# A decoder trunk in split float32 matmuls: five raw weight buffers for four, gate biases loaded into short-lived tiles, residual rows loaded in four portions

## The chip, the core and the metric

One core of a Trainium2 chip runs the whole kernel in one launch. The metric is the device time of one execution in microseconds (us); lower is better. TensorE (PE) multiplies matrices, VectorE (DVE), ScalarE (ACT) and GpSimd (POOL) do elementwise work, and SyncE (SP), ACT and POOL issue DMAs. Each engine runs its own instructions in the order in which they stand; semaphores hold an instruction until what it needs is there, and all that stands behind it on that engine waits too.

## The reference

The input `x` has 256 rows of 2048 channels (one batch, one layer), all in float32. What is computed:

```python
x = layer_norm(x, ln_in_g, ln_in_b)
z = x @ w_in                       # 2048 x 13312: a_b a_c a_h | b_u b_v | c_a c_g | g
gates = sigmoid(g + gate_bias).reshape(1, 256, 3, 2048)
y_a = a_b * causal_depthwise_conv(a_c * a_h, conv_a_w)              # 3 taps
y_b = b_u * (tril(sg_w) @ layer_norm(b_v) + sg_b)                   # chunks of 128 rows
y_c = silu(layer_norm(causal_depthwise_conv(c_a * sigmoid(c_g), cc_conv_w) + cc_conv_b))   # 31 taps
proj = stack([y_a, y_b, y_c]) @ w_branch                            # three of 1024 x 2048
mix = sum(gates * proj, over branches) @ w_out                      # 2048 x 2048
x = layer_norm(alpha * x + mix, ln_mix_g, ln_mix_b)
h_gate, h_up = split(x @ w_ffn_in)                                  # 2048 x 11264
ffn = (silu(h_gate) * h_up) @ w_ffn_out                             # 5632 x 2048
out = layer_norm(alpha * x + ffn, ln_ffn_g, ln_ffn_b)
```

The weights are read once, some 300 MB in all.

## The kernel before

**Tiles.** Every product has 256 rows of activations (two tiles `t` of 128) against weights that come in tiles of 128 x 1024 float32 (512 KB). A weight tile lands raw in `wraw` (L183, `RAW_BUFS` = 4 buffers). ScalarE copies it, rounded, to `whi` (L128), and VectorE takes the rest, `wlo` = `wraw` - `whi` (L130). Activations are split the same way into a high and a low part (`th`, `tl`; `yh`, `yl` for a branch's output). A product is three matmuls of 128 x 512: high by high, low by high, high by low (L251 to L253 in `gemm_block`, L205 to L207 in `gemm`). A raw buffer is free once its `wlo` is made; a split buffer (seven pairs, `SPLIT_BUFS`) once PE has used it. A plain step of one tile is 12 matmuls.

**Pairs.** In `gemm_block` some weight tiles are taken two at a time, with seven products in place of eight. For those, VectorE makes four sums of the two raw tiles first (`split_pair`, L142 to L153; in the trace L140, written to `tsum` and once back to `wraw`), and these are split too. The sums of the products (`tmp`) are put together on VectorE after the last pair (L296 to L299) and added to the other banks at the end of the block (`total`, L656).

**The order.** `plan` lists all 552 weight tiles in the order in which they are used. `pump(i)` (L192), called ahead of step `i`, records loads up to tile `i + DMA_AHEAD` and splits up to tile `i + SPLIT_AHEAD`. SP issues the loads, so the load of a tile waits on SP for the `wlo` of the tile four places earlier. Work that follows a block (transposes on PE into `th`, the gates, the residual) is put off by some steps with `defer`, whose clock counts steps, and runs between the steps of the next block; the causal convolution of branch C runs as background taps, two a step (L563). A scheduler then sets the final order on each engine.

**The places that matter here.** `branch` (L675) computes for each of three branches, in two halves, the gates (`gemm_block(("g", n, b))`) and the branch's projection (`("p", n, b)`). It loads two gate biases of 128 x 512 ahead of each gate block with DMAs on ACT's queue into `gb` (L681, two buffers of their own), adds them at the block's end (L685), and merges (`merged`, L702 to L705). `merged` is transposed (L310) for the output projection `("o", ...)`. Small row vectors are broadcast by POOL's DMAs into `tmp` tiles (`bcast`, L802 to L804); `tmp` is a pool of eight tiles of 128 x 512 that nearly all of the elementwise work shares. The rows of `x` for the residual are loaded again into `R` by eight POOL DMAs (`residual_rows`, L809 to L812), all recorded three steps into the `o` block, and `residual` (L820, L822) normalizes them there. `mix_residual` (L857, L858) does the like in the feed-forward part.

Of the kernel before, what the change touches and what calls it, by code (L numbers as in the profile page):

```python
# [8 lines left out]
F32 = mybir.dt.float32  # L9
# [3 lines left out]
ALU = mybir.AluOpType  # L13

P = 128
D = 2048
S = 256
NT = S // P
# [5 lines left out]
ALPHA = 2.0 ** 0.25  # L24
NW = 512
KT = 2
RAW_BUFS = 4
SPLIT_BUFS = 7
DMA_AHEAD = 5
SPLIT_AHEAD = 3  # L30
DEFER = 2
BACKGROUND = 2
# [9 lines left out]
SUMS_AT = 5  # L42
X_PAIRS = 2
LEAD = 6
ADDER = False

OFF_AB, OFF_AC, OFF_AH = 0, DA, 2 * DA
OFF_BU, OFF_BV = 3 * DA, 4 * DA
# [5 lines left out]
def trunk_kernel(ctx: ExitStack, tc: tile.TileContext, x, ln_in_g, ln_in_b, w_in, gate_bias,  # L54
                 conv_a_w, sg_ln_g, sg_ln_b, sg_w, sg_b, cc_conv_w, cc_conv_b, cc_ln_g, cc_ln_b,
                 w_branch, w_out, ln_mix_g, ln_mix_b, w_ffn_in, w_ffn_out, ln_ffn_g, ln_ffn_b, out):
    nc = tc.nc
# [6 lines left out]
    small = ctx.enter_context(tc.tile_pool(name="small", bufs=4))  # L64
# [10 lines left out]
    x2d = x.rearrange("b s d -> (b s) d")  # L75
    out2d = out.rearrange("b s d -> (b s) d")

    def cols(j, w=NW):
        return slice(j * w, (j + 1) * w)

    def new_tmp():
        return tmp.tile([P, NW], F32, name="tmp")
# [50 lines left out]
    def split_pair(t0, t1):  # L133


        b12, b11, b22, b21 = t0[:, 0, :], t0[:, 1, :], t1[:, 0, :], t1[:, 1, :]
        ts = wp.tile([P, 3, NW], F32, name="tsum", bufs=1)

        def add(out, a, b):
            nc.vector.tensor_tensor(out=out, in0=a, in1=b, op=ALU.add)  # L140

        add(ts[:, 0, :], b11, b12)  # L142
        if ADDER:
            nc.gpsimd.dma_start(out=b12, in_=b22, accum_op=ALU.add)
        else:
            add(b12, b12, b22)
        add(ts[:, 1, :], ts[:, 0, :], b22)
        second = split_tile(t1)
        if ADDER:
            nc.scalar.copy(out=ts[:, 2, :], in_=ts[:, 1, :])  # L150
            nc.gpsimd.dma_start(out=ts[:, 2, :], in_=b21, accum_op=ALU.add)
        else:
            add(ts[:, 2, :], ts[:, 1, :], b21)  # L153
        low = split_tile(ts[:, 0:2, :])
        first = split_tile(t0)
        last = split_tile(ts[:, 2:3, :], 1)

        def part(pair, i):
            return pair[0][:, i, :], pair[1][:, i, :]

        return {"b11": part(first, 1), "t3": part(first, 0), "b22": part(second, 0), "b21": part(second, 1),
                "t1": part(low, 0), "t2": part(low, 1), "t4": part(last, 0)}
# [18 lines left out]
    def load_one():  # L181
        j = state["dma"]
        t = wp.tile([P, KT, NW], F32, name="wraw", bufs=RAW_BUFS)  # L183
        nc.sync.dma_start(out=t, in_=plan[j])
# [7 lines left out]
    def pump(i):  # L192

        while state["dma"] < min(len(plan), i + 1 + DMA_AHEAD):
            while state["dma"] - state["split"] >= RAW_BUFS:
# [16 lines left out]
    def defer(fn, after=DEFER, banks=True):  # L212


        deferred.append((clock[0] + after, fn, banks))
# [36 lines left out]
        nc.tensor.matmul(ps, lhsT=ah, rhs=bl, start=False, stop=False)  # L252
        nc.tensor.matmul(ps, lhsT=al, rhs=bh, start=False, stop=last)  # L253

    def gemm_block(key, xs, evac, combos=None):

        steps = block[key]
        xh, xl = xs  # L260
        pairs = sum(kind == "pair" for kind, _, _ in steps)
        outs = {at: acc_bank() for at in ((0, 1), (1, 1), (0, 0), (1, 0))}
        adds, shared, free_at = {}, None, 0

        def a_of(k, t):
            return xh[:, k, cols(t, P)], xl[:, k, cols(t, P)]

        def c_of(i, c):
            return combos[0][:, c, i, :], combos[1][:, c, i, :]

        for s_, (kind, q, tile_) in enumerate(steps):
            pump(tile_)
            b = split_t.pop(tile_)
            first, last = s_ == 0, s_ == len(steps) - 1
            if kind == "one":
                hi, lo = b
                for i, ((t, n), ps) in enumerate(outs.items()):
                    product(ps, a_of(q, t), (hi[:, n, :], lo[:, n, :]), first, last)
                    if last:
                        evac(i, t, n, ps, adds.get((t, n)))  # L280
            else:
                if q == 0:
                    shared = [halves[1].tile([P, NW], F32, name="acc") for _ in range(4)]
                p1, p5, p6, p7 = shared
                st, sp = q == 0, q == pairs - 1
                product(outs[0, 1], a_of(2 * q + 1, 0), b["b21"], first, last)
                product(outs[0, 0], c_of(q, 3), b["b22"], first, last)
                product(p5, c_of(q, 0), b["t1"], st, sp)
                product(p6, c_of(q, 1), b["t2"], st, sp)
                product(p1, a_of(2 * q, 0), b["b11"], st, sp)  # L290
                product(p7, c_of(q, 2), b["t3"], st, sp)
                product(outs[1, 1], a_of(2 * q + 1, 1), b["t4"], first, last)
                if sp:
                    c1, u, r, v, w = (new_tmp() for _ in range(5))
                    nc.scalar.copy(out=c1, in_=p1)
                    nc.vector.tensor_tensor(out=u, in0=p6, in1=c1, op=ALU.add)  # L296
                    nc.vector.tensor_tensor(out=r, in0=p5, in1=u, op=ALU.subtract)
                    nc.vector.tensor_tensor(out=v, in0=u, in1=p7, op=ALU.subtract)
                    nc.vector.tensor_tensor(out=w, in0=p7, in1=r, op=ALU.add)  # L299
                    adds = {(0, 1): c1, (1, 1): v, (0, 0): r, (1, 0): w}  # L300
                    free_at = s_ + 3
            clock[0] += 1 if kind == "one" else 2
            run_deferred(shared is not None and not 0 < free_at <= s_ and not last)
        halves.reverse()
# [23 lines left out]
        nc.gpsimd.tensor_tensor(out=rs, in0=r, in1=mhalf, op=ALU.pow)  # L328
        return mv[:, 0:1], rs

    def stats_tile(name, n):
        return [small.tile([P, n, 6], F32, name=f"{name}{t}", bufs=1) for t in range(NT)]


    wi = w_in[0]
# [49 lines left out]
    xpool = xin.enter_context(tc.tile_pool(name="xpool", bufs=1))  # L385
# [76 lines left out]
    xT = new_xt(act)  # L462
# [5 lines left out]
    xTS = new_sums()  # L468
    x_kept = [blocks(xpool.tile([P, NW], F32, name=f"xk{t}")) for t in range(NT)]
    def x_stats(t):  # L470
        st = small.tile([P, 4, 6], F32, name="st", bufs=2)
        for q in range(4):
            nc.vector.bn_stats(out=st[:, q, :], in_=xt[t][:, cols(q)])
        return mean_rstd(st, mv_in[t], rs_in[t])
# [24 lines left out]
    brp = None  # L499
# [108 lines left out]


    vt = {(t, j): brp.tile([P, NW], F32, name="gate", bufs=4) for t in range(NT) for j in range(2)}  # L610
    bst = stats_tile("bst", 2)
    for j in range(2):
        def evac_bv(t, ps, j=j):
            nc.scalar.copy(out=vt[t, j], in_=ps)
# [60 lines left out]
    def branch(n, y, first, mT=None):  # L675
        for b in range(2):
            gates = {}
            gb = [brp.tile([P, NW], F32, name="gb", bufs=2) for _ in range(2)]
            for i in range(2):
                o = n * D + (2 * b + i) * NW  # L680
                nc.scalar.dma_start(out=gb[i], in_=gate_bias[0:1, o:o + NW].broadcast_to([P, NW]))  # L681

            def evac_g(i, t, h, ps, add):
                g = gates[t, h] = brp.tile([P, NW], F32, name="gate", bufs=4)
                nc.vector.tensor_tensor(out=g, in0=total(ps, add), in1=gb[h], op=ALU.add)  # L685
                nc.scalar.activation(out=g, in_=g, func=AF.Sigmoid)

            gemm_block(("g", n, b), xT, evac_g, xTS)
            if b == 1 and mT is not None:
                mT.extend(new_xt(act))  # L690
                mTS.extend(new_sums())
                later = late[:]
                late.clear()
                for i, f in enumerate(later):
                    f(DEFER + i)

            def evac_p(i, t, h, ps, add):
                j = 2 * b + h
                m = merged[t][:, cols(j)]
                z = gates[t, h]  # L700
                if first:
                    nc.vector.tensor_tensor(out=m, in0=ps, in1=z, op=ALU.mult)  # L702
                else:
                    nc.vector.tensor_tensor(out=z, in0=ps, in1=z, op=ALU.mult)
                    nc.vector.tensor_tensor(out=m, in0=m, in1=z, op=ALU.add)  # L705
                if mT is not None:
                    def move(after):
                        to_left(mT, mTS, j, t, m, after)
                    if b == 0:
                        late.append(move)  # L710
                    else:
                        move(DEFER + i)

            gemm_block(("p", n, b), y(), evac_p)
# [74 lines left out]
    R, x2T, xS = [], [], []  # L789
# [16 lines left out]

    stm = stats_tile("stm", 4)
    lg2, lb2 = (a.rearrange("(o d) -> o d", o=1) for a in (ln_in_g, ln_in_b))
    def residual_rows():  # L809
        for j in range(4):  # L810
            for t in range(NT):
                nc.gpsimd.dma_start(out=R[t][:, cols(j)], in_=x2d[cols(t, P), cols(j)])  # L812

    def residual(j, wait):
        gj, bj = bcast(lg2, j), bcast(lb2, j)
# [25 lines left out]
            for q in range((S_PAIRS + 1) // 2):  # L841
                defer(lambda q=q: token_sums(xS, 2 * q, kept[0, q], kept[1, q], min(2, S_PAIRS - 2 * q)), 6 + q, False)

    defer(residual_rows, 3, False)
    for j, at in enumerate((5, 7, 15, 17)):
        defer(lambda j=j: residual(j, 4), at, False)
    gemm_block(("o", 0), mT, lambda i, t, h, ps, add: evac_o(t, h, ps, add), mTS)
# [11 lines left out]
        defer(go, 3, False)  # L859


    stf = stats_tile("stf", 4)
    f_ln = {}

    def silu(ps, add=None):
# [96 lines left out]
```

## Time and profile before

| what | value |
|---|---|
| median of 3 runs | 1554.5 us (1552.83 to 1554.87) |
| the profiled execution's own time | 1554.82 us |
| its span, first to last instruction | 1553.1 us |
| PE busy | 1522.3 us, 98% |
| DVE, ACT, POOL busy | 1340.4 (86%), 771.2 (50%), 33.9 us (2%) |
| DMA | 308 MB, mean 198 GB/s |
| granted TensorE clock, mean | 0.995 |

A row of the timeline has the start, how long the instructions took, the engine, line, operation, what it writes and reads, a count and, in brackets, how long the engine stood idle before it and what ended that. `<-DMA wraw` means that a weight tile had not landed; `<-ACT whi` and `<-DVE wlo` that its high or low part was not made. The trace calls a buffer by its name in the kernel. An engine that is idle costs nothing unless PE, or the end, waits for it.

### The profile page before, as it was taken

Reading aid. Unit: us, or ns where it says so; the run is one execution under the profiler, and the core shown is the slowest. Engines: PE = TensorE matmul, PEld = TensorE weight load, DVE = VectorE, ACT = ScalarE, POOL = GpSimd, SP = SyncE. Lnnn points to the kernel's source line nnn. Section 1 sums busy time; section 2 is a strip of 40 time slices with the busy share of each in tenths; the row PEclk is TensorE's granted clock in tenths of the full one; section 3 lists DMA queues with packets and bytes.
Section 4 is the critical chain, followed back from the end, with each engine's and each line's share of the span. In section 5 each row is a group of like instructions: output and inputs, shape, how many; then the busy total and the mean of one; then the engine's idle time right before and its main releaser. Section 6 shows DMA issues by size and latency. Waiting matters only on the chain. (4 is left out here: it accounts for less than half of the span.)

```text
span 1553.1 us, 18820 instructions
## 1 busy us (share of the span) xinstructions
PE 1522.3 (98%) x6799; PEld 1246.5 (80%) x6799; DVE 1340.4 (86%) x1792; ACT 771.2 (50%) x885; POOL 33.9 (2%) x60
## 2 busy tenths in 40 slices
PE   7999999999999999999999999999999999999997
PEld 5888888888888888887877888788888878888885
DVE  7699999978789878787789799988899988888677
ACT  5544445444455454545436455555555554455451
POOL 1000000000000000000101000000000000000001
PEclk9999999999999999999999999999999999999998
DMA  6866556566664665756765666566665666666654
GB/s 221 271 190 189 183 153 227 169 216 205 197 204 156 213 204 185 243 170 201 235 208 182 203 190 216 177 227 207 190 189 176 203 193 198 206 190 202 217 180 145
DMA packets 103315, 308.13 MB, mean 198 GB/s; under 512 B 9908, under 2 KB 11028, under 8 KB 103222
## 3 DMA queue, kind: packets, MB, share of 16 engines
q1 hardware_dynamic: 98006, 293.29, 60.0%
q0 software_dynamic: 2560, 8.39, 1.9%
q10 hardware_dynamic: 2656, 5.26, 1.1%
q8 instruction: 53, 0.87, 0.2%
q14 instruction: 40, 0.33, 0.1%
HBM read 304.80 MB, written 2.10 MB: 198 GB/s over the span
## 5 line engine op out<-in xcount | busy, mean ns | idle before, releaser
L128 ACT CAST whi<-wraw 128x1024 fp32r<-128x1024 f32 x551 | 577.1, 1052 | 537.2 <-PE acc L253 165.7
L130 DVE TENSOR_TENSOR wlo<-wraw,whi 128x1024 fp32r<-128x1024 f32 x551 | 667.3, 1222 | 125.1 <-ACT whi L128 121.0
L251 PE MATMUL acc<-whi,th 128*128 128x512 f32 x1235 | 485.9, 393 | 1.9 <-ACT th L316 1.0
L252 PE MATMUL acc<-wlo,th 128*128 128x512 f32 x1235 | 481.7, 390 | 0.0
L253 PE MATMUL acc<-whi,tl 128*128 128x512 f32 x1235 | 481.1, 390 | 0.4 <-DVE tl L317 0.4
L251 PEld LDWEIGHTS acc<-whi,th 128*128 128x128 f32 x1235 | 231.9, 188 | 51.1 <-ACT th L316 1.4
L253 PEld LDWEIGHTS acc<-whi,tl 128*128 128x128 f32 x1235 | 231.7, 188 | 51.3 <-DVE tl L317 1.4
L252 PEld LDWEIGHTS acc<-wlo,th 128*128 128x128 f32 x1235 | 232.1, 188 | 47.8 <-DVE wlo L130 0.2
L205 PE MATMUL acc<-whi,th 128*128 128x512 f32 x496 | 195.4, 395 | 0.5 <-ACT whi L128 0.4
L206 PE MATMUL acc<-wlo,th 128*128 128x512 f32 x496 | 194.4, 393 | 1.6 <-DVE wlo L130 1.6
L207 PE MATMUL acc<-whi,tl 128*128 128x512 f32 x496 | 194.0, 392 | 0.0
L128 ACT CAST whi<-tsum 128x1024 fp32r<-128x1024 f32 x114 | 95.3, 836 | 145.4 <-DVE tsum L140 116.1
L130 DVE TENSOR_TENSOR wlo<-tsum,whi 128x1024 fp32r<-128x1024 f32 x114 | 108.7, 953 | 13.4 <-ACT whi L128 13.4
L206 PEld LDWEIGHTS acc<-wlo,th 128*128 128x128 f32 x496 | 93.5, 189 | 22.0 <-DVE wlo L130 3.0
L205 PEld LDWEIGHTS acc<-whi,th 128*128 128x128 f32 x496 | 93.6, 189 | 20.8 <-ACT whi L128 1.2
L207 PEld LDWEIGHTS acc<-whi,tl 128*128 128x128 f32 x496 | 93.6, 189 | 20.1 <-DVE tl L317 0.4
L563 DVE SCALAR_TENSOR_TENSOR cv<-pad,cw,cv 128x256 f32<-128x256 f32 x240 | 101.9, 489 | 0.0
L140 DVE TENSOR_TENSOR tsum<-tsum,wraw 128x512 f32<-128x512 f32 x114 | 78.2, 686 | 0.6
L251 PE MATMUL acc<-whi,yh 128*128 128x512 f32 x192 | 75.7, 394 | 0.0
L252 PE MATMUL acc<-wlo,yh 128*128 128x512 f32 x192 | 75.5, 393 | 0.0
L253 PE MATMUL acc<-whi,yl 128*128 128x512 f32 x192 | 74.7, 389 | 0.0
L140 DVE TENSOR_TENSOR tsum<-wraw 128x512 f32<-128x512 f32 x57 | 39.2, 688 | 32.6 <-DMA wraw<-in_w_in_dram 20.8
(164 smaller groups left out, 1191.1 us busy)
## 6 DMA issues: line engine op xcount, KB each, us to landing
wraw<-in_w_in_dram SPq DMA_DIRECT2D x208, 512.0 KB, 4.1
wraw<-in_w_ffn_in_dram SPq DMA_DIRECT2D x176, 512.0 KB, 4.3
wraw<-in_w_ffn_out_dram SPq DMA_DIRECT2D x88, 512.0 KB, 4.7
wraw<-in_w_branch_dram SPq DMA_DIRECT2D x48, 512.0 KB, 5.0
wraw<-in_w_out_dram SPq DMA_DIRECT2D x32, 512.0 KB, 6.4
gb<-in_gate_bias_dram ACTq DMA_DIRECT2D x12, 256.0 KB, 3.8
R<-in_x_dram POOLq DMA_DIRECT2D x8, 256.0 KB, 8.2
x<-in_x_dram SPq DMA_DIRECT2D x2, 512.0 KB
```

What stands on the lines that cost most here:

```text
L128: nc.scalar.copy(out=hi, in_=t)
L130: nc.vector.tensor_tensor(out=lo, in0=t, in1=hi.bitcast(F32), op=ALU.subtract)
L140: nc.vector.tensor_tensor(out=out, in0=a, in1=b, op=ALU.add)
L205: nc.tensor.matmul(ps, lhsT=xh[:, k, ts], rhs=hi[:, kk, :], start=first, stop=False)
L206: nc.tensor.matmul(ps, lhsT=xh[:, k, ts], rhs=lo[:, kk, :], start=False, stop=False)
L207: nc.tensor.matmul(ps, lhsT=xl[:, k, ts], rhs=hi[:, kk, :], start=False, stop=last)
L251: nc.tensor.matmul(ps, lhsT=ah, rhs=bh, start=first, stop=False)
L252: nc.tensor.matmul(ps, lhsT=ah, rhs=bl, start=False, stop=False)
L253: nc.tensor.matmul(ps, lhsT=al, rhs=bh, start=False, stop=last)
L563: nc.vector.scalar_tensor_tensor(out=cv[:, b, :], in0=pad[:, b, q:q + S], scalar=w_, in1=cv[:, b, :], op0=ALU.mult, op1=ALU.add)
```

## The change

`RAW_BUFS` goes from 4 to 5 and `DMA_AHEAD` from 5 to 6. The gate biases lose their own tiles `gb`: they are loaded into two `tmp` tiles by POOL's DMAs, recorded after the last pair of the gate block (by a new argument `with_sums` of `gemm_block`) where they were recorded ahead of the block, on ACT's queue. The rows of `x` are recorded in four portions of two DMAs, at steps 2, 4, 8 and 10 of the `o` block. Some small statistics tiles move to other pools (`st` to `xpool`, `bst` to `brp`), and the last layer norm uses the tile of the one before (`stm`). A branch that no setting used (`ADDER`) goes. Line numbers in the changed kernel are 1 to 5 lower.

```diff
-RAW_BUFS = 4
+RAW_BUFS = 5
-DMA_AHEAD = 5
+DMA_AHEAD = 6
...
-    def gemm_block(key, xs, evac, combos=None):
+    def gemm_block(key, xs, evac, combos=None, with_sums=None):
...
                     adds = {(0, 1): c1, (1, 1): v, (0, 0): r, (1, 0): w}
                     free_at = s_ + 3
+                    if with_sums is not None:
+                        with_sums()
...
-        st = small.tile([P, 4, 6], F32, name="st", bufs=2)
+        st = xpool.tile([P, 4, 6], F32, name=f"st{t}")
...
-    bst = stats_tile("bst", 2)
+    bst = stats_tile("bst", 2, brp)
...
-            gb = [brp.tile([P, NW], F32, name="gb", bufs=2) for _ in range(2)]
-            for i in range(2):
-                o = n * D + (2 * b + i) * NW
-                nc.scalar.dma_start(out=gb[i], in_=gate_bias[0:1, o:o + NW].broadcast_to([P, NW]))
+            gb = []
+
+            def load_bias(o=n * D + 2 * b * NW):
+                for i in range(2):
+                    gb.append(new_tmp())
+                    nc.gpsimd.dma_start(out=gb[i], in_=gate_bias[0:1, o + i * NW:o + (i + 1) * NW].broadcast_to([P, NW]))
...
-            gemm_block(("g", n, b), xT, evac_g, xTS)
+            gemm_block(("g", n, b), xT, evac_g, xTS, load_bias)
...
-    def residual_rows():
-        for j in range(4):
-            for t in range(NT):
-                nc.gpsimd.dma_start(out=R[t][:, cols(j)], in_=x2d[cols(t, P), cols(j)])
+    def residual_rows(j):
+        for t in range(NT):
+            nc.gpsimd.dma_start(out=R[t][:, cols(j)], in_=x2d[cols(t, P), cols(j)])
...
-    defer(residual_rows, 3, False)
+    for j, at in enumerate((2, 4, 8, 10)):
+        defer(lambda j=j: residual_rows(j), at, False)
...
-    stf = stats_tile("stf", 4)
+    stf = stats_tile("stm", 4)
```

SP issues the same DMAs in the same order before and now. On VectorE, here is the stretch from the last half of branch C to `merged`, which PE transposes next. Names: `tl<-tmp` is the low part of an activation tile, L456 are sums of activation tiles, `tsum<-wraw` and `wraw<-wraw` are the first two sums of a pair of raw weight tiles. Before:

```order
L130 TENSOR_TENSOR wlo<-wraw,whi 128x1024
L317 TENSOR_TENSOR tl<-tmp,th 128x4x128
L130 TENSOR_TENSOR wlo<-wraw,whi 128x1024
L317 TENSOR_TENSOR tl<-tmp,th 128x4x128
L456 TENSOR_TENSOR tmp<-tmp 128x256 x3
L140 TENSOR_TENSOR tsum<-wraw 128x512
L456 TENSOR_TENSOR tmp<-tmp 128x256
L130 TENSOR_TENSOR wlo<-wraw,whi 128x1024
L460 TENSOR_TENSOR sum_5990<-tmp,sum_5989 128x512 x2
L704 TENSOR_TENSOR gate<-acc,gate 128x512 x2
```

The same stretch now:

```order
L129 TENSOR_TENSOR wlo<-wraw,whi 128x1024
L312 TENSOR_TENSOR tl<-tmp,th 128x4x128
L139 TENSOR_TENSOR tsum<-wraw 128x512
L129 TENSOR_TENSOR wlo<-wraw,whi 128x1024
L312 TENSOR_TENSOR tl<-tmp,th 128x4x128
L451 TENSOR_TENSOR tmp<-tmp 128x256 x3
L139 TENSOR_TENSOR wraw<-wraw 128x512
L451 TENSOR_TENSOR tmp<-tmp 128x256
L129 TENSOR_TENSOR wlo<-wraw,whi 128x1024
L455 TENSOR_TENSOR sum_5992<-tmp,sum_5991 128x512 x2
L701 TENSOR_TENSOR gate<-acc,gate 128x512 x2
```

The first sum of the pair has moved ahead of a `wlo`, a `tl` and three L456, and the second sum stands ahead of the merge where it stood behind it.

On POOL, here is what stands around the rows of `x` (`R`), from the statistics of branch C on. Before:

```order
L328 TENSOR_TENSOR rstd<-ve,mhalf 128x1 x2
L804 DMA tmp<-in_ln_in_g_dram 128x512
L804 DMA tmp<-in_ln_in_b_dram 128x512
L804 DMA tmp<-in_ln_in_g_dram 128x512
L804 DMA tmp<-in_ln_in_b_dram 128x512
L812 DMA R_6227<-in_x_dram 128x512
L812 DMA R_6228<-in_x_dram 128x512
```

Now:

```order
L323 TENSOR_TENSOR rstd<-ve,mhalf 128x1 x2
L678 DMA tmp<-in_gate_bias_dram 128x512 x8
L801 DMA tmp<-in_ln_in_g_dram 128x512
L801 DMA tmp<-in_ln_in_b_dram 128x512
L801 DMA tmp<-in_ln_in_g_dram 128x512
L801 DMA tmp<-in_ln_in_b_dram 128x512
L808 DMA R_6229<-in_x_dram 128x512
L808 DMA R_6230<-in_x_dram 128x512
```

Eight of the twelve gate biases stand there now (the other four ahead of the statistics). The eight DMAs of the rows of `x` stand one behind the other in both kernels, behind the same four broadcasts.

## Rows read from the trace of the kernel before

**Rows 1.** Windows: stretch, its length, busy time of each engine, granted clock, DMA.
```profile
50.00:1500.00 1450.00, 1439.38 (x6439) 1182.58 (x6438) 1260.90 (x1673) 728.40 (x823) 20.42 (x36) 1.00 0.63 198
```
**Rows 2.** Timeline of PE: an even matmul, and those that stood behind a wait.
```profile
466.48 0.39 PE L253 MATMUL acc<-whi,tl 128*128 128x512 f32 x1
467.54 0.50 PE L251 MATMUL acc<-whi,th 128*128 128x512 f32 x1 [0.67 <-ACT tok L572]
...
733.71 0.55 PE L310 MATMUL acc<-ident,merged 128*128 128x128 f32 x3 [2.42 <-DVE merged L705]
...
744.85 0.50 PE L253 MATMUL acc<-whi,tl 128*128 128x512 f32 x1 [0.44 <-DVE tl L317]
...
793.08 0.50 PE L206 MATMUL acc<-wlo,th 128*128 128x512 f32 x1 [0.48 <-DVE wlo L130]
...
804.62 0.50 PE L206 MATMUL acc<-wlo,th 128*128 128x512 f32 x1 [0.36 <-DVE wlo L130]
...
806.42 0.50 PE L205 MATMUL acc<-whi,th 128*128 128x512 f32 x1 [0.38 <-ACT whi L128]
...
807.68 0.50 PE L206 MATMUL acc<-wlo,th 128*128 128x512 f32 x1 [0.76 <-DVE wlo L130]
...
991.75 0.50 PE L251 MATMUL acc<-whi,xS 128*128 128x512 f32 x1 [0.54 <-ACT whi L128]
...
993.01 0.50 PE L252 MATMUL acc<-wlo,xS 128*128 128x512 f32 x1 [0.76 <-DVE wlo L130]
...
1275.10 0.50 PE L251 MATMUL acc<-whi,th 128*128 128x512 f32 x1 [0.97 <-ACT th L316]
```
**Rows 3.** Timeline of ACT: four splits that waited for their weight tile.
```profile
465.95 1.05 ACT L128 CAST whi<-wraw 128x1024 fp32r<-128x1024 f32 x1 [2.97 <-DMA wraw<-in_w_in_dram]
...
719.68 1.05 ACT L128 CAST whi<-wraw 128x1024 fp32r<-128x1024 f32 x1 [7.01 <-DMA wraw<-in_w_out_dram]
...
793.16 1.05 ACT L128 CAST whi<-wraw 128x1024 fp32r<-128x1024 f32 x1 [6.03 <-DMA wraw<-in_w_out_dram]
...
805.32 1.05 ACT L128 CAST whi<-wraw 128x1024 fp32r<-128x1024 f32 x1 [2.01 <-DMA wraw<-in_w_out_dram]
```
**Rows 4.** Timeline of DVE: the merge, and instructions that waited for weights.
```profile
728.48 0.69 DVE L140 TENSOR_TENSOR tsum<-wraw 128x512 f32<-128x512 f32 x1 [1.36 <-DMA wraw<-in_w_out_dram]
...
731.76 0.69 DVE L704 TENSOR_TENSOR gate<-acc,gate 128x512 f32<-128x512 f32 x1
...
968.70 0.69 DVE L140 TENSOR_TENSOR wraw<-wraw 128x512 f32<-128x512 f32 x1 [1.10 <-DMA wraw<-in_w_ffn_in_dram]
...
1255.70 1.23 DVE L130 TENSOR_TENSOR wlo<-wraw,whi 128x1024 fp32r<-128x1024 f32 x1 [2.02 <-ACT whi L128]
```
**Rows 5.** Timeline of SP: weight loads as they are issued.
```profile
704.94 0.33 SPq L184 DMA_DIRECT2D wraw<-in_w_out_dram  x1
...
710.88 0.33 SPq L184 DMA_DIRECT2D wraw<-in_w_out_dram  x1
...
723.75 0.33 SPq L184 DMA_DIRECT2D wraw<-in_w_out_dram  x1
...
780.96 0.37 SPq L184 DMA_DIRECT2D wraw<-in_w_out_dram  x1
...
789.27 0.37 SPq L184 DMA_DIRECT2D wraw<-in_w_out_dram  x1
```
**Rows 6.** By tile: who waited for `wraw`; landing times of all weight loads.
```profile
  DVE tsum L140: 32.2, 17
...
DMA to landing us min/median/max: 3.4/4.4/9.9
```
**Rows 7.** By tile and window: landing of the weight loads from 704 to 724.
```profile
DMA to landing us min/median/max: 9.0/9.1/9.1
```
**Rows 8.** By source L804: landing of POOL's broadcasts.
```profile
DMA to landing us min/median/max: 3.6/4.8/6.7
```
**Rows 9.** Timeline of POOL: the rows of `x`.
```profile
744.49 4.32 POOL L812 DMA_DIRECT2D R<-in_x_dram  x8 [33.55 <-PE acc L310]
```

More of the change, by code (lines that the diff above doesn't have):

```diff
@@ L44 @@
 LEAD = 6
-ADDER = False
 OFF_AB, OFF_AC, OFF_AH = 0, DA, 2 * DA
@@ L142, in split_pair @@
         add(ts[:, 0, :], b11, b12)
[L143 to L146, printed above, removed]
+        add(b12, b12, b22)
         add(ts[:, 1, :], ts[:, 0, :], b22)
         second = split_tile(t1)
[L149 to L153, printed above, removed]
+        add(ts[:, 2, :], ts[:, 1, :], b21)
         low = split_tile(ts[:, 0:2, :])
@@ L329, in mean_rstd, with stats_tile @@
         return mv[:, 0:1], rs
-    def stats_tile(name, n):
-        return [small.tile([P, n, 6], F32, name=f"{name}{t}", bufs=1) for t in range(NT)]
+    def stats_tile(name, n, pool=None):
+        return [(pool or small).tile([P, n, 6], F32, name=f"{name}{t}", bufs=1) for t in range(NT)]
     wi = w_in[0]
```

## The prediction

> **What bounds the kernel now.** I read the windows first. Between 50 and 1500 us PE is busy 1439.38 of 1450 us at the full granted clock [rows 1], so PE is the bound, and outside the load phase at the front and the last layer norm at the back there are 10.6 us of idle time for the whole change to win. Nothing in the change touches either end: the front waits for the first layer norm, and the chain of the last layer norm is the same. Its statistics now share a tile with those of the norm before, which were read some 700 us earlier.
>
> Next I read PE's timeline for the places at which that idle time lies. Each is a matmul with a bracket [rows 2]. A bracket understates the loss. A matmul is drawn 0.39 us long, but 6439 of them start in 1439.38 us, one every 0.22 [rows 1, 2]; full-width ones start 0.23 apart. So each wait costs its bracket and 0.16 us more. By that the ten with brackets lose: 467 0.83; 733 2.58; 744 0.60; 793 0.64; the three from 804 to 808 0.52, 0.54 and 0.92; the two at 991 and 993 0.70 and 0.92; 1275 1.13. Together 9.4 us (the row at 466 is an even one, ahead of the first wait). PE never waits for a DMA itself. What it waits for are ACT's and DVE's results, so the third view is what held these up: rows of ACT that stood behind a weight tile not yet landed [rows 3], and rows of DVE [rows 4].
>
> **The fifth buffer.** Before, the load of a tile waits on SP for the `wlo` of the tile four places earlier; now for the one five places earlier. A load is thus issued when its predecessor was issued before. It needs no new work. What it is worth at each of PE's waits:
>
> - 467: ACT stood 2.97 us until 465.95 behind a tile, and the copy of a transposed tile (`tok`) for which PE waits stands right behind that split [rows 2, 3]. One load earlier is about one plain step earlier (12 matmuls, 2.76 us), which leaves at most 0.2 of the 2.97. I count the whole 0.83.
> - 804 to 808: the tiles are late because their loads are. The one split at 793.16 was issued at 789.27 and would now go at 780.96, when its predecessor went [rows 3, 5]. It lands before ACT is free, and each of the five that follow takes the place of its predecessor, 2 to 3 us earlier; the split at 805.32, which waited 2.01 for its tile, goes at about 802.3. All three waits go: 1.98 us.
> - 793: PE waited for a `wlo` that stands behind the residual's work on DVE, not behind a tile. Bounds 0 and 0.64; I take 0, since DVE's order there is unchanged.
> - 991 and 993: DVE ran without a break to there from 968.70, where it had stood 1.10 us for the second raw tile of a pair [rows 4]. That tile now comes one load earlier, DVE's whole chain moves up by 1.10, and of PE's 1.62 us 0.5 remain. I count 1.10; bounds 0 and 1.62.
> - 1275: DVE stood 2.02 us until 1255.70 behind a split that waited for its tile [rows 4], and works on from there without a break to the transposes. What follows at 1256 also waits for PE's own pair to end, so not all 2.02 come forward. Bounds 0 and 1.13; I take the middle, 0.6.
> - 733 and 744: see below.
>
> The sum without the stretch from 733 on is 0.83 + 1.98 + 1.10 + 0.6 = 4.5 us.
>
> **The merge at 733.** This is the longest of PE's waits, and behind it is the longest of ACT's in these rows: 7.01 us for a tile of `w_out` issued at 710.88 [rows 2, 3, 5]. That load now goes at 704.94, so ACT's 7.01 us go for that tile. What is late next is the tile behind it, which takes over the 710.88. From 704 to 724 the loads took 9.0 to 9.1 us where 4.4 is the median [rows 6, 7], because POOL's four broadcasts of 256 KB are in flight with a burst of weight loads. A fifth load in that burst joins the line. ACT then waits again, until about 719.7 for the second tile, which it split at 721.1 before. So DVE's chain gains some 1.4 us, not 7.
>
> And the scheduler spends that. In DVE's new order two sums of the next pair, 0.6 us each as they follow each other (drawn 0.69 [rows 4]), stand ahead of the merge, and the first waits for a tile that was issued at 723.75 and is now issued at about 716 [rows 5]. From the first sum to L704 DVE took 3.28 us before [rows 4]. What now stands between them besides is a `wlo` of 1.2, the second sum of 0.6 and four narrower instructions, which I put at 1.6 (an estimate, by width from these two): 6.6 us in all. If the tile lands one tile behind the burst, near 725 (the burst's four loads went from 710.88 on, 1.1 us apart as the `wlo` that free them, so that the last landed about 9.1 after 714.3, at 723.4), DVE reaches L704 at 731.6, against 731.76 before. I count nothing at 733; the bounds are 2.58 won and 3.3 lost (the rivals). Behind the merge the two sums no longer stand in the way of `tl`, for which PE waited at 744.85: that chain is 1.2 us shorter, and 0.60 us go.
>
> The Trainium skill bears on this ("DMA: Bandwidth & Descriptors", section "Issuing engines are not separate DMA queues"): DMAs started on SP, ACT or POOL end up on the same 16 DMA engines and interleave. The 9.1 us against 4.4 agree with it [rows 6, 7]. By it a deeper line of loads doesn't shorten a burst; were it not so, the rival with the large gain would be the likeliest.
>
> **The gate biases.** Twelve issues of ACT go; ACT is busy 728 of 1450 us [rows 1], and PE waits for it only where a tile or a transpose is late, so this is worth 0. POOL gets twelve more, on an engine that is busy 20 of 1450 us. They are recorded three plain steps ahead of the first use: 3 x 2.76 = 8.3 us. In truth POOL is idle and issues as soon as the two `tmp` tiles are free, which by the order of use is when the adds of the gate block before, or the transposes early in the block, are done. But take the 8.3: broadcasts from POOL land in 3.6 to 6.7 us, 4.8 in the median [rows 8]. So even the slowest leaves 1.6 us. If one took the 9.9 us of the slowest weight load [rows 6], each of six blocks would lose 1.6, 9.6 in all; that is the upper bound, and 0 the lower. I take 0, by rows 8. Behind such a wait would stand DVE's adds and the next `wlo`. The two tiles less in `tmp` hurt nobody: the tile that the second sum takes in a block's end was freed on DVE itself by the first.
>
> **The rows of x.** On POOL the eight DMAs still stand together behind the same four broadcasts, and before they were issued in 4.32 us at 744.49 as soon as PE had read the last merged tile [rows 9]. This release hasn't moved, so recording them in four portions changes nothing: 0. Were they spread, the loads of `w_out` around 750 would land sooner, but PE has no wait between 744.85 and 793.08 [rows 2], so that too is worth 0.
>
> **Sum.** 4.5 + 0.6 = 5.1 us off the profiled execution's 1554.82 makes 1549.7. The median of the runs shown is 0.3 lower, so the forecast is 1549.4.
>
> **Rivals.**
>
> *A: the waits come back (1554).* The splits are earlier, but DVE, busy 1261 of 1450 us [rows 1], is the real second bound, and what it saves by waiting less it finds as other work. For it: at 793, 991 and 1275 the last to be late is DVE's own chain. Against it: at 467 and from 804 on the chain in the rows ends at a DMA. Only 467 is certain then: 1554.5 - 0.8 = 1553.7, and with a small new wait 1554.
>
> *B: the merge wait goes too (1545).* If the loads land 4 to 5 us after issue in spite of the burst, because the first of them now goes while nothing else is in flight, DVE reaches the merge some 3 us earlier and the 2.58 us go; with what I left at 793, 991 and 1275 (0.64 + 0.5 + 0.5) that is 4.2 more: 1545.2. Against it are the 9.1 us [rows 7].
>
> *C: slower, the sums moved ahead hold DVE (1558).* DVE now takes up the first sum of a pair ahead of splits that stood before it. If the pair's tile lands no earlier than before, everything behind it on DVE waits, the `wlo` of the present step included. At the merge: DVE is at the sum at about 722.5 (719.7, the split 1.05, its `wlo` 1.2 and a `tl`), and the tile landed at 728.4 before [rows 4]. With 5.9 us of waiting and then the 6.6 of work, the merge comes at about 735.1, and PE's wait there grows by 3.3: 1554.5 + 3.3 = 1557.8. The point from which it decides is a landing after 725. All 17 such waits together were 32.2 us before [rows 6], and PE felt none directly [rows 2], which speaks against more than that.
>
> *D: the portions don't do what they say.* That is my forecast for them, at no cost; it isn't counted apart.
>
> **How the numbers follow.** Forecast 0.53, A 0.25, B 0.11, C 0.11. A change of 0.2%, 3.1 us, is about what a measurement of this kernel can tell from none: faster means below 1551.4, slower above 1557.6. The forecast's own terms may miss by about 2 us (the bounds at 991, 1275 and 744), so of its 0.53 some 0.46 lie below 1551.4 and 0.07 within. With B that is 0.57 faster. A adds its 0.25 to within, which with half of C's cases at 1557.8 and below is 0.35; slower is the rest, 0.08. The range reaches down to B's 1545.2 and up over A to 1556.0; above it lies most of C, below it a part of B.
>
> **What would show it.** Right: no bracket on PE at 467 and from 804 to 808, one of half the size at 991, and the one at the merge as long as before; ACT's waits for `wraw` shorter in sum; the first wait for `w_out` at the merge gone and a like one on the tile behind it. The gate biases land ten or more us ahead of L682, and the eight rows of `x` go in one burst at the merge's transposes. Wrong: new brackets on PE behind `tsum` (C), behind a gate add (the biases), or PE's idle time between 50 and 1500 still about 10 us (A).

## The result and the profile after

| | runs | median us | lowest to highest |
|---|---|---|---|
| before, beside the changed kernel | 4 | 1553.66 | 1549.95 to 1554.87 |
| changed | 4 | 1544.74 | 1543.98 to 1545.0 |

The ratio is 0.9944, 95% interval 0.9932 to 0.9956: faster by 8.9 us, 0.5 us below the range that was forecast. The direction was right and the size too small. The kernel before is the restless one of the two: beside the experiments its median was 1550.35 (17 runs, 1547.83 to 1556.82), 1551.2 (19) and 1551.0 (9). The changed kernel with a recording depth of five, which is as fast as it, ran 5.4 us ahead of the first of these, so the change is worth some 5 to 9 us. The profiled execution of before, 1554.82, lies near the top, that of the changed kernel, 1543.98, at the bottom of its four, so the two profiles are 10.8 us apart (spans 11.2), more than the medians.

First the windows of the changed kernel, to be held against [rows 1].

```profile
50.00:1500.00 1450.00, 1448.61 (x6484) 1191.95 (x6482) 1274.45 (x1683) 735.63 (x829) 27.18 (x48) 1.00 0.64 200
```

PE is busy 1448.61 us in place of 1439.38; 1.4 us of idle time are left of 10.6. These are PE's rows of the changed kernel at the matmuls that waited before: at the copy behind 467, at the merge, at 793, at 806 and 807, and at 1275 (the names of lines are 1 to 8 lower than before).

```profile
466.06 0.39 PE L243 MATMUL acc<-whi,th 128*128 128x512 f32 x1
466.29 0.39 PE L244 MATMUL acc<-wlo,th 128*128 128x512 f32 x1
...
730.97 0.39 PE L245 MATMUL acc<-whi,tl 128*128 128x512 f32 x1
731.20 0.60 PE L305 MATMUL acc<-ident,merged 128*128 128x128 f32 x4
...
789.22 0.39 PE L198 MATMUL acc<-wlo,th 128*128 128x512 f32 x1
...
801.23 0.39 PE L197 MATMUL acc<-whi,th 128*128 128x512 f32 x1
801.46 0.39 PE L198 MATMUL acc<-wlo,th 128*128 128x512 f32 x1
...
1263.65 0.49 PE L243 MATMUL acc<-whi,th 128*128 128x512 f32 x1
```

No row has a bracket; every one of the ten waits of [rows 2] is gone. What is left behind 50 us are the layer norm's three brackets from 813 to 831 (0.78, 0.39 and 0.15 us), which stood in before too. The waits of ACT tell why. Before, then after (line, what it waited for: us in total, times, longest):

```profile
ACT whi L128 <- PE acc L253: 187.2, 166, 3.0
...
ACT whi L128 <- DMA wraw<-in_w_ffn_in_dram: 60.1, 49, 6.9
ACT whi L128 <- DMA wraw<-in_w_in_dram: 49.2, 37, 4.5
ACT whi L128 <- DMA wraw<-in_w_out_dram: 38.7, 18, 7.0
ACT whi L128 <- DMA wraw<-in_w_ffn_out_dram: 36.9, 28, 9.7
```

```profile
ACT whi L127 <- PE acc L245: 315.7, 279, 3.0
...
ACT whi L127 <- DMA wraw<-in_w_ffn_out_dram: 15.2, 11, 5.9
ACT whi L127 <- DMA wraw<-in_w_out_dram: 9.9, 5, 2.4
...
ACT whi L127 <- DMA wraw<-in_w_ffn_in_dram: 8.0, 11, 1.7
ACT whi L127 <- DMA wraw<-in_w_in_dram: 5.6, 7, 1.9
```

With four buffers ACT stood behind weight tiles that had not landed. With five it stands behind PE: the tiles are there, and it waits until PE has read the split tiles whose place it needs. That is the healthy state: a queue that is full behind the engine that bounds the kernel.

Where the 11.2 us came from, as the difference of PE's starts between the two traces, matmul for matmul (forecast: the terms on record). It holds for this pair of executions:

| place (us of before) | forecast | measured |
|---|---|---|
| front, to 30 | 0 | 1.2 |
| 226 | not named | 0.3 |
| 467 | 0.83 | 0.8 |
| spacing of matmuls, 230 to 718 | not named | -2.2 |
| merge, 733 and 744 | 0.60 | 3.1 |
| 793 and 804 to 808 | 1.98 | 3.1 |
| 991 to 1005 | 1.10 | 2.1 |
| 1259 to 1275 | 0.6 | 3.1 |
| end | 0 | -0.3 |

### The profile page after: what moved, and what is told of

Same layout as the page of the kernel before. It is cut to its first block, busy times and chain, and to the rows that moved or that the text cites. A ratio compares the mean times of both kernels' runs of the same rounds, so it can differ in the third digit from the quotient of the medians.

```text
span 1541.9 us, 18855 instructions
## 1 busy us (share of the span) xinstructions
PE 1522.0 (99%) x6799; PEld 1247.5 (81%) x6799; DVE 1343.1 (87%) x1792; ACT 771.6 (50%) x885; POOL 40.6 (3%) x72
## 4 chain that ended last, share of the span: by engine, by line
PE 86%; DVE 9%; issue 2%; DMA 1%; ACT 1%; POOL 0%; POOLq 0%; DVEq 0%; ACTq 0%
PE acc L243 24%; PE acc L245 24%; PE acc L244 24%; DVE cv L558 4%; PE acc L198 4%; PE acc L199 4%; PE acc L197 4%; DVE wlo L129 2%; PE acc L305 2%; DMA wraw<-in_w_in_dram 0%; DMA x<-in_x_dram 0%; POOL ve L320 0%; DVE st L468 0%; DVE tmp L635 0%; ACT whi L127 0%
## 5 line engine op out<-in xcount | busy, mean ns | idle before, releaser
L651 DVE TENSOR_TENSOR tmp<-acc,tmp 128x512 f32<-128x512 f32 x92 | 59.9, 683 | 0.6
```

The lines of the kernel that those rows point to most:

```text
L651: nc.vector.tensor_tensor(out=c, in0=ps, in1=add, op=ALU.add)
```

## The experiments

**Four buffers, the rest of the change.** 

```diff
-RAW_BUFS = 5
+RAW_BUFS = 4
-DMA_AHEAD = 6
+DMA_AHEAD = 5
```

> The changed kernel with four raw buffers and the issue depth of before; the late gate biases and the residual rows in four portions stay. Theory (the fifth buffer is all of it): the time of before, 1553.7 us (1550 to 1555), and between 50 and 1500 us PE is busy about 1439 us, with the waits at 467, 733, 744, 793, 804 to 808, 991 and 1275 back. Rival (the late gate biases, which leave ACT's queue, or the new order give a part): 1546 to 1550, and some of these waits stay away.

1552.89 (12 runs, 1549.56 to 1555.53), ratio to before 1.0009 (0.9999 to 1.002). The waits are back; its window, and two of PE's rows:

```profile
50.00:1500.00 1450.00, 1442.63 (x6445) 1184.10 (x6444) 1262.82 (x1674) 729.05 (x822) 28.58 (x48) 1.00 0.61 198
```

```profile
734.63 0.33 PE L305 MATMUL acc<-ident,merged 128*128 128x128 f32 x1 [0.45 <-DVE merged L702]
...
807.85 0.50 PE L198 MATMUL acc<-wlo,th 128*128 128x512 f32 x1 [0.77 <-DVE wlo L129]
```

Most sit at the same places with other sizes. At the merge it is 0.45 in place of 2.42, but `merged` was not made earlier: its transposes start at 734.63, against 733.71 in before. PE came there 2.9 us later than in before, by a longer wait at 226 (1.19 us in place of 0.38) and by wider spaced matmuls from 230 on (see below), and so waited less. What PE loses ahead of a starved place, the next wait gives back; this kernel's time doesn't show the spacing in full. Kernels with four buffers spread over 5 to 9 us and those with five over 1 to 3; that starved places, whose cost hangs on when a tile lands, are the reason was not shown by a run.

**The buffer alone.** Before, with `RAW_BUFS = 5`, `DMA_AHEAD = 6`, and the room from the pool of temporaries:

```diff
-    tmp = ctx.enter_context(tc.tile_pool(name="tmp", bufs=8))
+    tmp = ctx.enter_context(tc.tile_pool(name="tmp", bufs=6))
```

> The kernel before with five raw buffers and nothing else of the change: gate biases early on ACT's queue in tiles of their own, residual rows in one piece; two tmp tiles fewer (six) make the room. Theory (the fifth buffer is all of it): 1544.7 us (1543.5 to 1546), PE busy 1448 to 1449 us of the 1450 between 50 and 1500. Rival (the rest of the change gives a part): 1547 or more, with brackets on PE left in the gate blocks. A loss of its own from the two tmp tiles would show as new brackets behind tmp.

1544.96 (6 runs, 1543.8 to 1546.51), ratio 0.9958 (0.9945 to 0.9971); PE busy 1448.68 of the 1450 us. With the kernel of four buffers above, which gained nothing, the buffer is all of the gain. But the trace hides two terms that cancel: its last matmul starts 2.9 us earlier than the changed kernel's (1527.2 against 1530.1), and then the last layer norm takes 14.8 us in place of 11.8, since with six temporaries two of its broadcasts go at a time, not four. The 2.9 us are followed up below.

**Depth of recording.** In the changed kernel:

```diff
-DMA_AHEAD = 6
+DMA_AHEAD = 5
```

> The changed kernel with five raw buffers, but each load recorded one step later (a depth of five, as before). Theory (a load is held by its buffer, not by where it is recorded): 1544.7 us (1543.5 to 1546) and no bracket on PE at the merge. Rival (it is the deeper recording that issues the loads earlier): 1550 to 1554, with the bracket at 733 back.

1544.95 (6 runs, 1543.85 to 1545.36), PE busy 1448.49, no bracket at the merge. With five buffers a load is held by its buffer; the step from five to six in depth does nothing here.

**Three buffers.** In the changed kernel:

```diff
-RAW_BUFS = 5
+RAW_BUFS = 3
-DMA_AHEAD = 6
+DMA_AHEAD = 4
```

> The changed kernel with three raw buffers and a depth of four. PE's idle time between 50 and 1500 us was 10.6 us with four and 1.4 us with five. Theory (the buffers set how far the loads run ahead, and ACT's waits for raw tiles, 208 us with four and 42 with five, spread from a few places to everywhere): 1575 to 1610 us, with ACT waiting over 400 us for raw tiles. Rival (only the few places with a burst of other work matter, each by some 2.8 us more): about 1575 or less, and no new brackets outside these places.

1625.61 (4 runs, 1622.41 to 1627.51), more than either expected. ACT's longest waits for weight tiles:

```profile
ACT whi L127 <- DMA wraw<-in_w_in_dram: 198.9, 120, 6.7
ACT whi L127 <- DMA wraw<-in_w_ffn_in_dram: 180.3, 91, 8.1
ACT whi L127 <- DMA wraw<-in_w_ffn_out_dram: 105.1, 58, 9.7
```

With the rows of the two other weights they are 581 us in all (208 with four buffers, 42 with five), and 46 of PE's waits cost over 0.5 us (bracket and 0.16). Not all of the loss is waiting: behind a wait of 6.2 us at the merge the granted clock from 750 to 800 was 0.93, and the changed kernel has 1.00 from 400 to 800. From three to four buffers it is 73 us, from four to five 5 to 9. With five, 1.4 us of idle time are left between 50 and 1500, so a sixth could win little more of this kind; no run had six.

**What the branch matmuls lost.** In the stretch from 230 to 718 the changed kernel's matmuls with `yh` and `yl` start further apart than before's, with no wait anywhere. Three rows of each kernel, before first; between the first and the last lie six steps in before, seven in the changed one:

```profile
254.66 0.39 PE L252 MATMUL acc<-wlo,yh 128*128 128x512 f32 x1
254.89 0.39 PE L253 MATMUL acc<-whi,yl 128*128 128x512 f32 x1
...
256.04 0.39 PE L252 MATMUL acc<-wlo,yh 128*128 128x512 f32 x1
```

```profile
253.74 0.39 PE L243 MATMUL acc<-whi,yh 128*128 128x512 f32 x1
253.97 0.40 PE L244 MATMUL acc<-wlo,yh 128*128 128x512 f32 x1
...
255.37 0.40 PE L244 MATMUL acc<-wlo,yh 128*128 128x512 f32 x1
```

1.38 / 6 = 230 ns and 1.63 / 7 = 233 ns, at a granted clock of 1.00 in both. What differs is the place of `yh` and `yl` in memory, since the two `gb` tiles and `bst` moved. One unused tile puts them 128 bytes on:

```diff
         brp = br.enter_context(tc.tile_pool(name="brp", bufs=1))
+        nc.vector.memset(brp.tile([P, 32], F32, name="spare"), 0.0)
```

> The changed kernel with one unused tile of 128 bytes a partition at the head of the pool of the gate blocks, so that yh and yl, the stationary operands of the branch matmuls, lie at 0x31880 and 0x33880 in place of 0x31800 and 0x33800 (in the kernel before they lay at 0x30980 and 0x32980); nothing else moves by as much as one instruction. In the kernel before the starts of these matmuls are 230.3 ns apart for yh and 226.4 for yl, in the changed one 233.4 and 233.4, in the stretches 249 to 336, 510 to 596 and 640 to 728. Theory (the low bits of these addresses set the spacing, and the change has moved them): 230.3 and 226.4 again, about 2.5 us less, 1542.2 us. Rival (the late gate biases or the deeper loads slow these matmuls): 233.4 stays, 1544.7.

1542.02 (4 runs, 1541.59 to 1543.09), `yh` 230.3 and `yl` 226.4 ns. The time is where the theory put it. It also prices the gate biases: from 98 us to the last matmul this kernel and the one with the buffer alone, which loads them early on ACT's queue and whose `yh` has the same spacing, differ by 0.15 us.

**Own address or distance.** Two more kernels with a pad, the first in `small`, ahead of the gate and feed-forward pools, the second in `const`, ahead of everything:

```diff
+    nc.vector.memset(small.tile([P, 16], F32, name="spare", bufs=1), 0.0)
```

```diff
+    nc.vector.memset(const.tile([P, 16], F32, name="spare"), 0.0)
```

> The changed kernel with one unused tile of 64 bytes a partition ahead of the gate and feed-forward pools: th and tl of the feed-forward move from 0x26f80 to 0x26fc0, which has the low eight bits (0xc0) of the th of the gate blocks (0x18cc0, spacing 226.9 ns), xS by the same 64 bytes, yh and yl from 0x31800 to 0x31840. Theory (placement sets the spacing): feed-forward th falls from 229.3 to 226.9 and its tl from 228.4 to 227.2, xS from 229.4 to 226.7: 1122 x 2.4 + 566 x 1.2 + 216 x 2.7 ns = 4.0 us less, 1540.7; if the low seven bits decide, yh and yl fall from 233.4 to 226.7 as well, 570 x 6.7 = 3.8 us more, 1536.9. Rival (the spacing belongs to the work of the stage, not to addresses): 1544.7.

> The changed kernel with 64 unused bytes ahead of every pool: the split weights (moving operands) go from low eight bits 0xc0 to 0x00 and the gate blocks' th from 0xc0 to 0x00 with them; the feed-forward's th lies at 0x26fc0 and yh at 0x31840, as with the small pad. If the distance between the weights and the stationary operand decides: all spacings as in the changed kernel (gate th 226.9, feed-forward th 229.3, yh 233.4), 1544.7. If the stationary operand's own address decides: gate th, where most matmuls are, at 0x00 as yh was, rises from 226.9 to 233.4 (some 3000 matmuls with tl, 20 us), while the feed-forward falls: about 1557 to 1561.

1540.08 (6 runs, 1538.79 to 1541.32) and 1544.99 (6 runs, 1543.71 to 1546.5). In the second the gate blocks' `th` lies at 0x00 and keeps its 227.1 ns: its own address doesn't count. The feed-forward's `th`, at 0xc0 from the weights again, has 228.3. Here is the mean time from one full-width matmul's start to the next, over all that follow each other within 260 ns, by the distance of the stationary operand from the split weights, modulo 256 bytes:

| distance | operands, kernel | ns |
|---|---|---|
| 0x00 | `th` of the gate blocks, all kernels | 226.8 to 227.0 |
| 0x40 | `yh` and `yl`, changed, and with the pad ahead of everything | 233.2 to 233.4 |
| 0x80 | `yh` and `yl`, small pad | 232.4 and 232.3 |
| 0xc0 | `yh` and `yl`, before | 230.2 and 226.4 |
| 0xc0 | `th`, `tl` and `xS` of the feed-forward, before | 228.6, 227.8 and 228.9 |

The rows at 0xc0 show that this distance is not the whole rule: `yl` lies there as `yh` does and runs as fast as an operand at 0. What sets them apart stays open. The small pad brings the feed-forward's `th` to distance 0: 227.0. The other half of that expectation, that the low seven bits decide and `yh` falls to 226.7 as well, came out wrong: it has 232.4.

**The merge.** The kernel before, with broadcasts of 16 columns in its residual:

```diff
+    def thin(src, j):
+        t_ = new_tmp()
+        nc.gpsimd.dma_start(out=t_[:, 0:16], in_=src[0:1, j * NW:j * NW + 16].broadcast_to([P, 16]))
+        return t_[:, 0:1].broadcast_to([P, NW])
-        gj, bj = bcast(lg2, j), bcast(lb2, j)
+        gj, bj = thin(lg2, j), thin(lb2, j)
```

> The kernel before, in which the eight broadcasts of ln_in's gain and bias move 8 KB each in place of 256 KB (16 columns are loaded and the first of them is used for all, which leaves out the other columns of these two vectors). Theory of the prediction (POOL's broadcasts hold the burst of weight loads up, 9.0 us to landing): the loads from 710.88 on land in 5 to 6 us, ACT's wait of 7.0 us falls to about 3, and PE's bracket of 2.42 us at 733 falls under 0.6. Rival (with four buffers the loads start too late, broadcasts or not): landing still falls, but the bracket at 733 stays over 1.2, since the burst begins only with the wlo at 710.88.

1547.27 (10 runs, 1543.95 to 1549.92). Landing of two of the four loads from 710 on, against 9.0 to 9.1 in [rows 7] (each view has a landing time for the third and the fourth alone); ACT's wait, against 7.01 in [rows 3]; the first sum of the pair, against 728.48 in [rows 4]; and PE at the merge:

```profile
DMA to landing us min/median/max: 6.1/6.1/6.2
```

```profile
715.90 1.05 ACT L128 CAST whi<-wraw 128x1024 fp32r<-128x1024 f32 x1 [4.11 <-DMA wraw<-in_w_out_dram]
...
724.85 0.69 DVE L140 TENSOR_TENSOR tsum<-wraw 128x512 f32<-128x512 f32 x1 [1.51 <-DMA wraw<-in_w_out_dram]
...
730.79 0.38 PE L310 MATMUL acc<-ident,merged 128*128 128x128 f32 x2
```

No bracket at the merge, and PE is there earlier than in before, so it isn't a late PE that hides one. With four buffers, it is the broadcasts in flight that make the merge late, as the prediction read it. The waits at 467, from 801 on, at 1000 and at 1268 stay (0.86, 0.45 and 0.76, 1.27, 0.97), so the buffer does more than that.

**All operands at distance 0.** Both pads, 64 bytes in `small` and 128 in the gate blocks' pool, as in the diffs above. And the same kernel with one more edit:

```diff
-POOL_SPLIT = (0,)
+POOL_SPLIT = ()
```

> The changed kernel with both unused tiles: 64 bytes ahead of the gate and feed-forward pools and 128 more at the head of the gate blocks' pool, so that every stationary operand (th, tl, yh, yl, xS, sum) has the low eight bits of the split weights, 0xc0. Theory (the distance of the two operands modulo 256 bytes sets the spacing, and 0 is the best): yh and yl fall from 232.4 ns in the kernel with the small pad to 226.9, 571 x 5.5 ns = 3.1 us off its 1540.1: 1537.0 us, with all groups at 226.6 to 228.2. Rival (yh and yl are slow for another reason, such as their distance from each other): 1540.1.

> As the kernel with both unused tiles, but the low part of the very first weight tile is made by DVE in place of POOL. In the kernel before POOL's wlo (2.41 us from 9.38) ran beside DVE's second normalising instruction, which then took some 2.5 us in place of 0.54; in the changed kernel it began at 9.85, after it. Theory (the two clash whenever they overlap, and the changed kernel was lucky by 1.2 us at the front): the clash can't occur, DVE has 1.22 us more to do at the front, some of it on the way to PE: 0 to 1.2 us slower than with both pads in its best runs, with a narrower spread. Rival (the clash is of no account): 1.2 us slower in all.

1536.85 (4 runs, 1535.39 to 1537.74), ratio to before 0.9907 (0.9892 to 0.9922); `yh` and `yl` at 226.7 and 227.4 ns. The expectation was 1537.0: this version beats both kernels. The one without POOL's share: 1539.25 (5 runs, 1537.9 to 1540.12), 2.4 us slower, more than either side expected. DVE's `wlo` now stands between the two normalising instructions for which PE waits:

```profile
9.87 1.23 DVE L129 TENSOR_TENSOR wlo<-wraw,whi 128x1024 fp32r<-128x1024 f32 x1 [0.26 <-ACT whi L127]
```

1.5 us of the difference between the two traces lie before 36 us, 0.7 at 742, 0.3 later. POOL's share at the front is worth keeping.

## Why the prediction was too small

**The step that failed** is in the merge: "If the tile lands one tile behind the burst, near 725 ... I count nothing at 733". The rows of the changed kernel from the loads to the merge:

```profile
702.43 0.33 SPq L176 DMA_DIRECT2D wraw<-in_w_out_dram  x1
...
706.52 0.54 POOL L801 DMA_DIRECT2D tmp<-in_ln_in_g_dram  x1 [62.67 <-DVE tmp L651]
...
708.59 0.33 SPq L176 DMA_DIRECT2D wraw<-in_w_out_dram  x1
...
715.71 0.33 SPq L176 DMA_DIRECT2D wraw<-in_w_out_dram  x1
```

```profile
716.61 1.05 ACT L127 CAST whi<-wraw 128x1024 fp32r<-128x1024 f32 x1 [1.70 <-PE acc L245]
...
719.80 1.05 ACT L127 CAST whi<-wraw 128x1024 fp32r<-128x1024 f32 x1 [1.01 <-PE acc L245]
```

```profile
721.50 0.69 DVE L139 TENSOR_TENSOR tsum<-wraw 128x512 f32<-128x512 f32 x1 [1.98 <-DMA wraw<-in_w_out_dram]
...
728.13 0.68 DVE L701 TENSOR_TENSOR gate<-acc,gate 128x512 f32<-128x512 f32 x1
```

The pair's tile was issued at 715.71, where the prediction had "about 716". From the first sum to L701 DVE took 6.63 us; the prediction had 6.6. What failed is the landing: the sum could start at 721.50, 5.8 us after issue, not 9. The prediction kept before's burst and put one more load into it. But the burst looks like a sign of hunger itself: four loads in a row, 1.1 us apart, as ACT and DVE worked off tiles that had come late. Fed one load earlier, the second tile of `w_out` went at 702.43 (the forecast gave it its predecessor's 704.94), ahead of the broadcasts; three loads follow 1.1 us apart, then ACT waits for PE, and the loads go at PE's pace. PE's late arrival doesn't hide a wait here: in the kernel with the buffer alone it is at the merge 2.9 us earlier (728.30) and doesn't wait either. This reading of the burst rests on the rows and on the thin broadcasts, which shorten the landing with four buffers; no run held the issue times and changed the burst alone.

The rivals: B, the one with this outcome, had a chance of 0.11 and the time 1545.2. C, the sums moved ahead, hinged on a landing after 725; DVE did stand 1.98 us there, but at 721.5. A fell: nothing came back.

**Right by its own steps:** 467 (0.83, measured 0.8). The gate biases at 0: landing 4.4 us in the median, and 0.15 us in the comparison above. The depth and the rows of `x` at 0: recorded in one piece or in four they make the same program, instruction for instruction, and the eight DMAs go in one go again:

```profile
741.95 4.23 POOL L808 DMA_DIRECT2D R<-in_x_dram  x8 [32.98 <-PE acc L305]
```

**Right in mechanism, too small in size:** 793 to 808 (1.98, measured 3.1), 991 (1.10 and 2.1 with 1004.80), 1275 (0.6 and 1.3; 3.1 with the two waits ahead of it that the list lacked). Each took one DMA wait from one row and left the rest of PE's wait standing, as the work of a chain that had not moved. But the chain was late by all the waits ahead of it, and all of these went. The list was short as well: PE's waits at 226, 1004.80, 1260.51 and 1262.30 of the kernel before weren't in it, 2.2 us by the same measure. Two rows of before that should have stood in [rows 2]:

```profile
1260.51 0.50 PE L251 MATMUL acc<-whi,th 128*128 128x512 f32 x1 [0.23 <-DVE tmp L299]
...
1262.30 0.33 PE L310 MATMUL acc<-ident,a 128*128 128x128 f32 x1 [0.83 <-DVE a L873]
```

**Not seen at all:** the spacing, 2.2 us lost, by where the tiles came to lie; and 1.2 us at the front, which the kernel before can gain too (below), so that it can't be put down to the change. That the time came out as close to the range as 0.5 us is luck in part: with the spacing of before the changed kernel has 1542.02, and the forecast misses by 7.4 us in place of 4.7.

## What to carry to other kernels

When a load queue is one buffer too short, don't price its waits one at a time: look at what the engine that consumes the tiles waits for (DMA or the bound), and if a buffer turns the one into the other, all of PE's waits behind these tiles may go, as they did here. A burst of loads in the profile can be the catching up after such a wait; don't carry its landing times over to a kernel that is fed earlier. Whenever a change adds or drops a tile, compare the spacing of matmuls in the stretches without waits, for a shift of addresses alone was worth 2 to 8 us here.

## What the runs showed of the hardware

The start-to-start time of full-width matmuls changed with the distance of the stationary from the moving operand modulo 256 bytes: 226.7 to 227.4 ns at 0 (in the gate, branch and feed-forward blocks), 226.4 to 230.2 at 0xc0 by operand, 232.4 at 0x80, 233.4 at 0x40, the granted clock at 1.00 throughout. Over all stages that is the step from 1544.7 to 1536.9. Only multiples of 64 bytes were tried, and a pad moves an operand against all that lies ahead of it, not against the weights alone; that the weights count, PE's other operand, is the likeliest reading. The Trainium skill ("SBUF — State Buffer", section "SBUF: two separate sides") says that on the side of the engines only the port pair of DVE and GpSimd causes contention and that PE never waits on anyone. The spacing shows that PE's rate is not free of where its operands lie. Whether its own two reads meet each other or another engine has a part in it was not tested.

At the front DVE and POOL got into each other's way. Before, then after: DVE's two normalising instructions, and POOL's `wlo` of the first weight tile.

```profile
9.04 3.03 DVE L432 TENSOR_SCALAR tmp<-x,mvin,rsin 128x512 f32<-128x512 f32 x2 [1.00 <-POOL rsin L328]
...
9.38 2.41 POOL L175 TENSOR_TENSOR wlo<-wraw,whi 128x1024 fp32r<-128x1024 f32 x1 [0.37 <-ACT prm L427]
```

```profile
8.90 1.00 DVE L427 TENSOR_SCALAR tmp<-x,mvin,rsin 128x512 f32<-128x512 f32 x2 [1.01 <-POOL rsin L323]
...
9.85 2.35 POOL L167 TENSOR_TENSOR wlo<-wraw,whi 128x1024 fp32r<-128x1024 f32 x1 [0.98 <-ACT prm L422]
```

Where POOL began before DVE's second instruction, as here and with four buffers and the rest of the change (9.21), that instruction ended some 2 us later, when POOL was done; where POOL began at 9.64 or later, in all the other profiles with POOL's share, the two took 1.00. Where it began at 9.64, while DVE's second ran (the small pad), POOL's own took 2.62 in place of 2.35. Which comes first hangs on when the first weight tile lands: ACT could split it at 8.26 and 8.09 in the two profiles with the clash, and at 8.52 or later in the others, though its load is issued at 2.16 or 2.17 in all of them. Before with thin broadcasts, which has four buffers, is without the clash as well, so it doesn't take the change to avoid it; whether more loads at the start make the first tile later was not tested. The same section of the Trainium skill gives an exclusive lock of that port pair, held by whichever starts first for the whole instruction; these rows agree with it. That this is the whole 1.2 us of the front was not tested by a run.
